# Merge and MLP tail of a two-block model: pair sums on GpSimd, norms as steps between products, the last 512 tokens as two quarters

## The chip, the cores and the metric

One core of one Trainium2 chip runs the whole program. The metric is device time in microseconds (us), the median of the runs shown. TensorE is PE in the rows, VectorE DVE, ScalarE ACT, GpSimd POOL, and SP is the queue of SyncE, which issues most of the DMAs.

## The reference, cut to what matters

The model has two blocks on 1024 tokens of width 1024, all in float32. The change touches only the end of the second block: the gated merge of four branches, and the MLP.

```python
merged = jnp.zeros_like(x)
for i in range(N_BRANCHES):                       # 4 branches of width 256
    gate = jax.nn.sigmoid(h @ w_gate[i] + b_gate[i])
    merged = merged + gate * (branches[i] @ w_branch_up[i])
x = x + rms_norm(merged @ w_out, norm_mix_post)
h2 = rms_norm(x, norm_mlp_pre)
u = jax.nn.relu(h2 @ w_mlp_in)                    # 1024 -> 4096
x = x + rms_norm((u * u) @ w_mlp_out, norm_mlp_post)
```

## The kernel before

Activations are kept transposed: a page is 128 features by 512 tokens, so the 1024 tokens are two halves, and a matrix of width 1024 is 8 pages in each half. Float32 accuracy comes from splitting each operand into a high and a low part in a faster matmul format. `split` (L101) writes the high part on ACT and the low part (source minus high) on DVE; `mm3` (L111) then makes three matmuls of each product (lines L113, L114, L115). A product of one output page from 8 weight blocks, which `fm` (L167) makes, is so 24 matmuls of 512 columns. Weights come in pieces of 128 x 1024 by `wload` (L144): a DMA into one of two `raw` buffers, then the split into one of two `whi` and two `wlo`.

`merge` (L1755) works as follows. `branch_parts` (L1743) loads the 8 pages that the branches left in DRAM for one half into buffers named Y and splits them into pages named H (32 of them in all). Then `up(f)` makes output page f of the half, for f from 0 to 7: `gates` (L1764) loads the four gate pages of the NEXT f into Y buffers, four short products (6 matmuls each) go to PSUM, DVE multiplies each with (1 + gate) (L1780) into a further Y buffer and adds it to the sum so far (L1782), and the sum is split (L107 on ACT, L108 on DVE) into M pages. There are 16 Y buffers. The first half's eight `up` run alone; the second half's eight `up` alternate with the eight `proj` (L1788) of the first half, each 24 matmuls with `w_out2`, whose result ACT copies out and squares for the norm. Then `norms(0)` (L1797), the eight `proj` of the second half, and `norms(1)`.

`norms` needs the sum of squares over features: `rnorm` (L209) sums over partitions with matmuls against a column of ones (L198), takes the power -1/2 on POOL (L141) and spreads the result over the partitions with further matmuls (L206). Then for each of 8 pages: load the old page (tag `xo`, two buffers, L1802), scale (L1803), add the old page on DVE (L1804), store (L1805). `norm_half` (L807) squares the new pages, makes a second `rnorm`, and `h_pages` (L216) scales and splits each into H pages, the input of the MLP.

`fill` (L942) makes left-over gate products where TensorE would wait. When `merge` begins, two are left, and `self.fill(2)` at L1811 uses them up, so the `self.fill(1)` in the loop finds none, before the change as after it.

`mlp` (L1825) goes through the 32 hidden pages in 8 chunks of 4: `hidden` makes a chunk's pages (24 matmuls per page and half, then ReLU squared and a split), `project` (L1849) multiplies them with `w_mlp_out` and adds into 16 Y pages (L1862). The last chunk goes half by half: while `hidden` of the second half runs, `finish(0)` (L1870) norms the first half's output and stores it (L1883), in four steps between the four products. After the last product `finish(1)` does the same for the second half, with nothing beside it.

The program is written in the order above, but the order on each engine is made by a scheduler that lists an instruction as soon as its inputs and its buffer are due by its own reckoning, earlier program text first. Each engine, and SP, then works through its list in order: an instruction whose input is late holds up what stands behind it.

## Time and profile before

| what | us |
|---|---|
| median of 3 runs (3504.82 to 3507.55) | 3505.5 |
| the profiled execution, its own time | 3508.32 |
| its span, first to last instruction | 3506.5 |
| merge, first `up` to the MLP's first stretch without a wait (2572.9 to 2810) | 237.1 |
| MLP from there to the last matmul (2810 to 3486.1) | 676.1 |
| after the last matmul (3486.1 to the end) | 20.4 |

The page lists TensorE as busy 96% of the span. The times of one stretch are read as follows: the matmuls in it, times the distance at which they follow each other where nothing holds them up, against the length of the stretch; the difference is what TensorE lost there.

### The profile page before, as it was taken

What the parts mean: (1) busy time and instruction counts of PE and PEld (TensorE: products, weight loads), DVE (VectorE), ACT (ScalarE), POOL (GpSimd) and SP (SyncE); (2) the same over time, 40 slices, a digit from 0 to 9 for tenths busy, and PEclk for the clock granted to TensorE, in tenths of its full rate; (3) what the DMA queues carried; (4) which work ended last, traced back from release to release, by engine and by line L of the source; (5) the groups of instructions that cost most, each with busy time, mean ns of one, the idle gap of its engine ahead of it and who ended that gap; (6) DMA issues with size and microseconds to landing.
All of it is one profiled execution on the core that took longest, in us unless ns stands there. A gap on an engine that the chain in (4) does not pass through costs nothing.

```text
span 3506.5 us, 45207 instructions
## 1 busy us (share of the span) xinstructions
PE 3369.9 (96%) x18181; PEld 2812.7 (80%) x18181; DVE 1966.9 (56%) x3418; ACT 1321.3 (38%) x2106; POOL 109.2 (3%) x132
## 2 busy tenths in 40 slices
PE   7999999999999999999999999999989899999997
PEld 5888988777888888787777777779768788888886
DVE  6767644556767644565664367453477743333336
ACT  4656412334655312443312345463233442222222
POOL 0000000000000000000100000000000000000000
PEclk9999999999999999999999999999999999999998
DMA  5111111452111111443231211122275421111114
GB/s 185 57 36 51 50 55 57 140 179 86 48 43 36 41 46 63 158 162 119 87 95 65 67 55 56 49 70 75 85 256 178 158 89 48 48 49 49 49 61 149
DMA packets 138707, 302.34 MB, mean 86 GB/s; under 512 B 23944, under 2 KB 41336, under 8 KB 137984
## 3 DMA queue, kind: packets, MB, share of 16 engines
q1 hardware_dynamic: 129280, 282.65, 24.7%
q10 hardware_dynamic: 9216, 16.78, 1.3%
q8 instruction: 143, 2.34, 0.3%
q14 instruction: 68, 0.56, 0.1%
HBM read 245.30 MB, written 58.28 MB: 87 GB/s over the span
## 4 chain that ended last, share of the span: by engine, by line
PE 83%; DVE 5%; issue 5%; ACT 3%; DMA 3%; POOL 1%; SPq 0%; DVEq 0%; POOLq 0%; ACTq 0%
PE mm L113 21%; PE mm L114 21%; PE mm L115 21%; PE lg L388 2%; PE lg L389 2%; PE tp L512 2%; PE pv L113 1%; PE pv L206 1%; PE pv L114 1%; PE pv L115 1%; DMA S<-mix 1%; PE tp L198 1%; DVE wlo L105 1%; PE tp L1392 1%; ACT whi L104 1%
## 5 line engine op out<-in xcount | busy, mean ns | idle before, releaser
L113 PE MATMUL mm<-H,whi 128*128 128x512 f32 x2400 | 958.2, 400 | 26.9 <-DVE S L369 5.0
L115 PE MATMUL mm<-H,wlo 128*128 128x512 f32 x2400 | 949.4, 396 | 5.9 <-DVE wlo L105 5.7
L114 PE MATMUL mm<-H,whi 128*128 128x512 f32 x2400 | 949.8, 396 | 2.1 <-DVE H L105 2.1
L104 ACT CAST whi<-raw 128x1024 fp32r<-128x1024 f32 (+1 forms) x340 | 334.4, 984 | 860.3 <-PE mm L114 768.7
L105 DVE TENSOR_TENSOR wlo<-raw,whi 128x1024 fp32r<-128x1024 f32 (+1 forms) x340 | 387.4, 1140 | 421.6 <-ACT whi L104 409.9
L113 PEld LDWEIGHTS mm<-H,whi 128*128 128x128 f32 x2400 | 456.5, 190 | 125.5 <-ACT H L107 7.2
L115 PEld LDWEIGHTS mm<-H,wlo 128*128 128x128 f32 x2400 | 455.7, 190 | 104.2 <-DVE wlo L105 12.3
L114 PEld LDWEIGHTS mm<-H,whi 128*128 128x128 f32 x2400 | 456.2, 190 | 92.7 <-DVE H L105 2.9
L113 PE MATMUL mm<-whi,H 128*128 128x256 f32 x960 | 277.2, 289 | 3.9 <-DVE S L576 3.2
L114 PE MATMUL mm<-wlo,H 128*128 128x256 f32 x960 | 274.6, 286 | 3.1 <-DVE wlo L105 3.1
L115 PE MATMUL mm<-whi,H 128*128 128x256 f32 x960 | 273.7, 285 | 0.0
L113 PE MATMUL mm<-M,whi 128*128 128x512 f32 x640 | 249.5, 391 | 1.7 <-ACT whi L104 1.5
L115 PE MATMUL mm<-M,wlo 128*128 128x512 f32 x640 | 249.7, 390 | 0.2 <-DVE wlo L105 0.2
L114 PE MATMUL mm<-M,whi 128*128 128x512 f32 x640 | 249.5, 390 | 0.0
L113 PEld LDWEIGHTS mm<-whi,H 128*128 128x128 f32 x960 | 184.6, 192 | 6.8 <-issue 4.2
L114 PEld LDWEIGHTS mm<-wlo,H 128*128 128x128 f32 x960 | 184.8, 193 | 5.1 <-DVE wlo L105 4.2
L115 PEld LDWEIGHTS mm<-whi,H 128*128 128x128 f32 x960 | 184.6, 192 | 0.4
L489 DVE CUSTOM_DVE_ANT_0 lg<-lg,strip 128x1024 f32<-128x1024 f32 x128 | 155.2, 1234 | 25.8 <-PE lg L389 25.6
L1862 DVE TENSOR_TENSOR Y<-Y,mm 128x512 f32<-128x512 f32 x112 | 77.0, 687 | 159.1 <-PE mm L115 159.0
L493 ACT ACTIVATE L<-lg,mx 128x1024 f32<-128x1024 f32 x128 | 142.7, 1118 | 36.5 <-DVE mx L489 30.3
L113 PEld LDWEIGHTS mm<-M,whi 128*128 128x128 f32 x640 | 120.2, 188 | 28.0 <-ACT whi L104 1.9
L115 PEld LDWEIGHTS mm<-M,wlo 128*128 128x128 f32 x640 | 120.5, 188 | 25.6 <-DVE wlo L105 0.6
(455 smaller groups left out, 4968.0 us busy)
## 6 DMA issues: line engine op xcount, KB each, us to landing
raw<-in_w_in SPq DMA_DIRECT2D x106, 512.0 KB, 3.6
raw<-in_w_out SPq DMA_DIRECT2D x48, 512.0 KB, 4.0
raw<-in_w_gate SPq DMA_DIRECT2D x46, 512.0 KB, 3.5
raw<-in_w_mlp_in SPq DMA_DIRECT2D x40, 512.0 KB, 3.3
raw<-in_w_mlp_out SPq DMA_DIRECT2D x40, 512.0 KB, 3.2
Y<-gates SPq DMA_DIRECT2D x64, 256.0 KB, 5.0
gates<-gs ACTq DMA_DIRECT2D x60, 256.0 KB, 2.0
mix<-S SPq DMA_DIRECT2D x48, 256.0 KB, 2.1
```

The source lines that it names most:

```text
L104: nc.scalar.copy(hi, src)
L105: nc.vector.tensor_tensor(out=lo, in0=src, in1=hi.bitcast(F32), op=ALU.subtract)
L113: mm(out, lh, rh, start=start, stop=False)
L114: mm(out, lh, rl, start=False, stop=False)
L115: mm(out, ll, rh, start=False, stop=stop)
L198: self.nc.tensor.matmul(ss[:, n * i + j:n * i + j + 1], acc[:, j * P:(j + 1) * P], self.one, start=True, stop=True)
L388: mm(out, Q[m][qb // 4][:, sl], KH[m][half][:, o:o + kn], start=True, stop=False)
L389: mm(out, Q[m][qb // 4][:, sl], KL[m][half][:, o:o + kn], start=False, stop=not more)
L489: nc.vector.tensor_tensor_reduce(out=lg, in0=lg, in1=strip[:, w0:w0 + 1024], op0=ALU.add, op1=ALU.min, scale=-1.0, scalar=3.0e38, accum_ou ...
L493: nc.scalar.activation(pm, lg, AF.Exp, bias=mx, scale=-1.0, accum_out=sm)
L512: nc.tensor.transpose(tp[:, j, :], pm[:, kb * P:(kb + 1) * P], self.ident)
L1862: nc.vector.tensor_tensor(out=Y[d][half], in0=Y[d][half], in1=pt, op=ALU.add)
```

## The change

Seven things change, all in `merge` and `mlp`:

- `up` multiplies in place, in the gate's own Y buffer. Products 1 and 3 are added to 0 and 2 on GpSimd, and DVE adds the two pair sums. Each `up` so asks for 4 Y buffers in place of 8.
- The old pages of a half are fetched into 8 H buffers by `olds`, and no longer through 2 `xo` buffers.
- `norms` becomes ten steps (`first`, four `add`, `second`, four `scale`); the add of the old page moves to GpSimd, and the squares are taken page by page.
- The first half's steps run between the `proj` of the second half, as (3, 2, 0, 1, 1, 1, 1, 1) after each; the second half's run in the MLP, between the products of `hidden` and `project` of chunk 0 of the first half.
- `finish` takes the statistics in its first step, works on any columns of a half, and sends every second output page from ACT's queue.
- The last weights (4 pieces) are split into H pages (`last_weights`), not into `whi` and `wlo`.
- The last half's products are made for 256 tokens, then for the other 256, with the norm of the first quarter in steps inside the second.

```diff
@@ -180,12 +180,12 @@
             self.mm3(out, xh[:, sl], xl[:, sl], w[k][0], w[k][1], k == 0, k == nk - 1)
-    def sumsq_add(self, acc, src, first, scale=1.0, tag=("sq", 2)):
+    def sumsq_add(self, acc, src, first, scale=1.0, tag=("sq", 2), n=512):
         nc = self.nc
         if first:
             nc.scalar.activation(acc, src, AF.Square, scale=scale)
         else:
-            t = self.T(*tag)
+            t = self.T(*tag)[:, 0:n]
             nc.scalar.activation(t, src, AF.Square, scale=scale)
             nc.vector.tensor_tensor(out=acc, in0=acc, in1=t, op=ALU.add)
@@ -1756,7 +1756,7 @@
         nc = self.nc
-        res = []
+        res = [{} for _ in range(8)]
         M = [{} for _ in range(8)]
         G = {}
@@ -1772,17 +1772,16 @@
             hs = slice(half * 512, half * 512 + 512)
             gates(half * 8 + f + 1)
             w = self.wload(self.seg("w_up", f * 1024, 8, 128), 8, 128)
-            acc = None
-            for i, g in enumerate(G.pop(half * 8 + f)):
+            ts = G.pop(half * 8 + f)
+            for i, t in enumerate(ts):
                 pt = self.ps("mm")
                 self.fm(pt, w[2 * i:2 * i + 2], B[i], half)
-                t = self.T("Y", 16)
-                nc.vector.scalar_tensor_tensor(out=t, in0=g, scalar=1.0, in1=pt, op0=ALU.add, op1=ALU.mult)
-                if acc is not None:
-                    nc.vector.tensor_tensor(out=t, in0=t, in1=acc, op=ALU.add)
-                acc = t
+                nc.vector.scalar_tensor_tensor(out=t, in0=t, scalar=1.0, in1=pt, op0=ALU.add, op1=ALU.mult)
+                if i % 2:
+                    nc.gpsimd.tensor_tensor(out=t, in0=t, in1=ts[i - 1], op=ALU.add)
+            nc.vector.tensor_tensor(out=ts[3], in0=ts[3], in1=ts[1], op=ALU.add)
             hi, lo = self.T("M", 32, F32R), self.T("M", 32, F32R)
-            self.split(hi, lo, acc, scale=0.5)
+            self.split(hi, lo, ts[3], scale=0.5)
             M[f][half] = (hi, lo)
         def proj(f, half, ys, acc):
@@ -1794,16 +1793,37 @@
             self.sumsq_add(acc, y, f == 0)
             ys.append(y)
-        def norms(half, ys, acc):
+        def olds(half):
+            xo = [self.hp.tile([P, 512], F32, tag="H", bufs=32, name=self.nm("xo")) for _ in range(8)]
+            for f in range(8):
+                nc.sync.dma_start(out=xo[f], in_=self.x2[f * P:(f + 1) * P, half * 512:half * 512 + 512])
+            return xo
+
+        def norms(half, ys, acc, xo):
+
             hs = slice(half * 512, half * 512 + 512)
-            r = self.rnorm(acc, 1.0 / 1024.0)
-            for f in range(8):
-                xo = self.T("xo", 2)
-                nc.sync.dma_start(out=xo, in_=self.x2[f * P:(f + 1) * P, hs])
-                nc.vector.scalar_tensor_tensor(out=ys[f], in0=ys[f], scalar=self.n2[:, 8 + f:9 + f], in1=r, op0=ALU.mult, op1=ALU.mult)
-                nc.vector.tensor_tensor(out=ys[f], in0=ys[f], in1=xo, op=ALU.add)
-                nc.sync.dma_start(out=self.x3[f * P:(f + 1) * P, hs], in_=ys[f])
-            res.append(self.norm_half(ys, self.n2[:, 16:24]))
+            r = []
+
+            def first():
+                r.append(self.rnorm(acc, 1.0 / 1024.0))
+
+            def add(f0):
+                if f0 == 0:
+                    r.append(self.T("acc", 2))
+                for f in (f0, f0 + 1):
+                    nc.vector.scalar_tensor_tensor(out=ys[f], in0=ys[f], scalar=self.n2[:, 8 + f:9 + f], in1=r[0], op0=ALU.mult, op1=ALU.mult)
+                    nc.gpsimd.tensor_tensor(out=ys[f], in0=ys[f], in1=xo[f], op=ALU.add)
+                    nc.sync.dma_start(out=self.x3[f * P:(f + 1) * P, hs], in_=ys[f])
+                    self.sumsq_add(r[1], ys[f], f == 0)
+
+            def second():
+                r.append(self.rnorm(r[1], 1.0 / 1024.0))
+
+            def scale(f0):
+                for f in (f0, f0 + 1):
+                    res[f][half] = self.h_pages(ys[f], r[2], self.n2[:, 16 + f:17 + f])
+            pairs = range(0, 8, 2)
+            return [first] + [lambda f=f: add(f) for f in pairs] + [second] + [lambda f=f: scale(f) for f in pairs]
         ys, accs = [[], []], [self.T("yacc", 2) for _ in range(2)]
         B = self.branch_parts(br, 0)
@@ -1811,18 +1831,19 @@
         self.fill(2)
         for f in range(8):
             up(f, B, 0)
-            self.fill(1)
+            self.fill((1, 1, 1, 1, 1, 2, 1, 0)[f])
         B = self.branch_parts(br, 1)
         for f in range(8):
             up(f, B, 1)
             proj(f, 0, ys[0], accs[0])
-        norms(0, ys[0], accs[0])
+        steps = deque(norms(0, ys[0], accs[0], olds(0)))
         for f in range(8):
             proj(f, 1, ys[1], accs[1])
-        norms(1, ys[1], accs[1])
-        return self.pair_halves(res)
-
-    def mlp(self, H, out):
+            for _ in range((3, 2, 0, 1, 1, 1, 1, 1)[f]):
+                steps.popleft()()
+        return res, norms(1, ys[1], accs[1], olds(1))
+
+    def mlp(self, H, steps, out):
         nc = self.nc
@@ -1842,11 +1863,11 @@
                     hi, lo = self.T("M", 32, F32R), self.T("M", 32, F32R)
                     self.split(hi, lo, t)
                     U[j][half] = (hi, lo)
-                if between:
-                    between[j]()
+                for fn in between[j:j + 1]:
+                    fn()
             return U
-        def project(ch, U, halves):
+        def project(ch, U, halves, between=()):
             for dp in range(4):
                 w = self.wload(self.seg("w_mlp_out", (ch * 4 + dp) * 1024, 4, 256), 4, 256)
                 for dd in range(2):
@@ -1860,6 +1881,8 @@
                             nc.scalar.copy(Y[d][half], pt)
                         else:
                             nc.vector.tensor_tensor(out=Y[d][half], in0=Y[d][half], in1=pt, op=ALU.add)
+                for fn in between[dp:dp + 1]:
+                    fn()
         def olds(half):
             X = [self.T("M", 32) for _ in range(8)]
@@ -1867,30 +1890,66 @@
                 nc.sync.dma_start(out=X[d], in_=self.x3[d * P:(d + 1) * P, half * 512:half * 512 + 512])
             return X
-        def finish(half, X):
-
-            hs = slice(half * 512, half * 512 + 512)
-            acc = self.T("yacc", 2)
+        def finish(half, X, c0=0, n=512):
+
+            cs, os = slice(c0, c0 + n), slice(half * 512 + c0, half * 512 + c0 + n)
+            acc = self.T("yacc", 2)[:, 0:n]
             for d in range(8):
-                self.sumsq_add(acc, Y[d][half], d == 0)
-            r = self.rnorm(acc, 1.0 / 1024.0)
+                self.sumsq_add(acc, Y[d][half][:, cs], d == 0, n=n)
+            r = []
             def scale(d0):
+                if d0 == 0:
+                    r.append(self.rnorm(acc, 1.0 / 1024.0))
                 for d in (d0, d0 + 1):
-                    y = Y[d][half]
-                    nc.vector.scalar_tensor_tensor(out=y, in0=y, scalar=self.n2[:, 24 + d:25 + d], in1=r, op0=ALU.mult, op1=ALU.mult)
-                    nc.vector.tensor_tensor(out=y, in0=y, in1=X[d], op=ALU.add)
-                    nc.sync.dma_start(out=out[d * P:(d + 1) * P, hs], in_=y)
+                    y = Y[d][half][:, cs]
+                    nc.vector.scalar_tensor_tensor(out=y, in0=y, scalar=self.n2[:, 24 + d:25 + d], in1=r[0], op0=ALU.mult, op1=ALU.mult)
+                    nc.vector.tensor_tensor(out=y, in0=y, in1=X[d][:, cs], op=ALU.add)
+                    (nc.scalar if d % 2 else nc.sync).dma_start(out=out[d * P:(d + 1) * P, os], in_=y)
             return [lambda d=d: scale(d) for d in range(0, 8, 2)]
-        for ch in range(last):
-            for halves in ((0,), (1,)) if ch == 0 else ((0, 1),):
-                project(ch, hidden(ch, halves), halves)
+        def last_weights():
+
+            W = []
+            for dp in range(4):
+                raw = self.wp.tile([P, 4, 256], F32, tag="raw", bufs=N_RAW, name=self.nm("raw"))
+                nc.sync.dma_start(out=raw, in_=self.seg("w_mlp_out", (last * 4 + dp) * 1024, 4, 256))
+                W.append([])
+                for k in (0, 2):
+                    hi, lo = (self.hpage().rearrange("p (k n) -> p k n", n=256) for _ in range(2))
+                    self.split(hi, lo, raw[:, k:k + 2, :])
+                    W[dp] += [(hi[:, i, :], lo[:, i, :]) for i in range(2)]
+            return W
+
+        def quarter(W, U, half, c0, steps):
+            cs = slice(c0, c0 + 256)
+            Uq = [{half: tuple(t[:, cs] for t in u[half])} for u in U]
+            for d in range(8):
+                pt = self.ps("mm")[:, 0:256]
+                self.fm(pt, [tuple(t[:, d % 2 * P:d % 2 * P + P] for t in w) for w in W[d // 2]], Uq, half)
+                y = Y[d][half][:, cs]
+                nc.vector.tensor_tensor(out=y, in0=y, in1=pt, op=ALU.add)
+                if d in (2, 3, 4, 5) and steps:
+                    steps[d - 2]()
+
+        def both(*fns):
+            def run():
+                for fn in fns:
+                    fn()
+            return run
+
+        U = hidden(0, (0,), [both(*steps[0:3]), both(*steps[3:5]), both(), steps[5]])
+        project(0, U, (0,), steps[6:])
+        project(0, hidden(0, (1,)), (1,))
+        for ch in range(1, last):
+            project(ch, hidden(ch, (0, 1)), (0, 1))
         project(last, hidden(last, (0,)), (0,))
         U = hidden(last, (1,), finish(0, olds(0)))
-        X = olds(1)
-        project(last, U, (1,))
-        for fn in finish(1, X):
+        X, W = olds(1), last_weights()
+        quarter(W, U, 1, 0, ())
+        steps = finish(1, X, 0, 256)
+        quarter(W, U, 1, 256, steps)
+        for fn in finish(1, X, 256, 256):
             fn()
     def second_block(self, H, out, end_banks):
@@ -1922,8 +1981,8 @@
                 self.fill(len(self.fills) - NLATE)
             end_banks()
             with self.banks("tail", 4, 0, 1, 2), self.phase("tail"):
-                H2 = self.merge(brd)
-                self.mlp(H2, out)
+                H2, steps = self.merge(brd)
+                self.mlp(H2, steps, out)
 def _woff():
```

## Rows read from the trace of the kernel before

**Rows 1.** Stretches: PE, PEld, DVE, ACT, POOL busy (instructions), PEclk, DMA share, GB/s

```profile
2572.90:2621.60 48.70, 45.29 (x192) 35.48 (x192) 47.03 (x70) 14.89 (x21) 0.00 (x0) 1.00 0.88 306
2621.60:2628.20 6.60, 0.75 (x3) 0.19 (x2) 6.34 (x10) 2.82 (x5) 0.00 (x0) 0.92 0.94 311
2628.20:2634.20 6.00, 6.00 (x14) 4.50 (x15) 5.96 (x10) 3.64 (x8) 0.00 (x0) 0.52 0.94 357
2634.20:2720.90 86.70, 86.70 (x384) 71.57 (x382) 62.75 (x86) 30.84 (x40) 0.00 (x0) 1.00 0.51 164
2720.90:2760.00 39.10, 34.29 (x155) 27.50 (x155) 27.76 (x41) 17.59 (x27) 2.01 (x2) 0.96 0.55 176
2760.00:2810.00 50.00, 45.89 (x208) 36.68 (x207) 38.19 (x57) 23.42 (x36) 2.01 (x2) 0.97 0.47 157
2810.00:3440.00 630.00, 629.85 (x2778) 520.91 (x2776) 241.61 (x304) 152.65 (x210) 0.00 (x0) 1.00 0.18 60
3440.00:3463.70 23.70, 22.86 (x101) 18.61 (x100) 17.66 (x27) 6.47 (x9) 1.01 (x1) 0.93 0.46 158
3486.10:3506.50 20.40, 3.14 (x17) 2.75 (x16) 11.71 (x19) 0.63 (x1) 1.01 (x1) 0.61 0.27 103
```

**Rows 2.** DVE in order of time, inside one `up` of the first half

```profile
2601.39 1.22 DVE L105 TENSOR_TENSOR wlo<-raw,whi 128x1024 fp32r<-128x1024 f32 x1
2602.53 0.68 DVE L1782 TENSOR_TENSOR Y<-Y,Y 128x512 f32<-128x512 f32 x1
2603.13 1.87 DVE L1780 SCALAR_TENSOR_TENSOR Y<-Y,mm 128x512 f32<-128x512 f32 x3
2604.93 0.68 DVE L108 SCALAR_TENSOR_TENSOR M<-Y,M 128x512 fp32r<-128x512 f32 x1
```

**Rows 3.** TensorE's waits, 2621.6 to 2634.2: total us, times, longest

```profile
PE mm L113 <- ACT H L104: 3.7, 1, 3.7
```

**Rows 4.** SP's queue in order of time: start, us, line, transfer

```profile
2585.42 0.90 SPq L1802 DMA_DIRECT2D xo<-x  x2
...
2621.16 3.97 SPq L1750 DMA_DIRECT2D Y<-br  x8
```

**Rows 5.** GpSimd's groups by shape, whole span: count, busy us, mean ns, idle before

```profile
L141 POOL TENSOR_TENSOR l<-l,mhalf 128x16 f32<-128x16 f32 x4 | 12.4, 3111 | 141.0 <-DVE l L140 141.0
L362 POOL MEMSET S<- 64x512 f32 x16 | 8.3, 521 | 17.1 <-PE lg L388 6.3 <-DVE N L219 3.3 <-ACT L L104 2.9
```

**Rows 6.** TensorE's waits, 2720.9 to 2760: total us, times, longest

```profile
PE tp L198 <- DVE acc L190: 1.8, 1, 1.8
PE pv L206 <- POOL rn L141: 1.3, 2, 0.8
```

**Rows 7.** TensorE's waits, 2760 to 2810

```profile
PE mm L115 <- DVE wlo L105: 1.8, 1, 1.8
```

**Rows 8.** DVE's waits, 2720.9 to 2810

```profile
DVE Y L1804 <- DMA xo<-x: 4.9, 6, 1.5
```

**Rows 9.** TensorE in order of time: the first norm's sums over partitions

```profile
2720.87 1.05 PE L198 MATMUL tp<-one,yacc 128*128 128x1 f32 x8
2721.78 0.48 PE L114 MATMUL mm<-M,whi 128*128 128x512 f32 x1
```

**Rows 10.** One stretch of products with 256 columns (columns as in the first group)

```profile
2434.60:2457.20 22.60, 22.60 (x190) 22.60 (x190) 1.18 (x2) 2.96 (x5) 0.00 (x0) 1.00 0.15 48
```

**Rows 11.** TensorE in order of time, after the last product: the norm's broadcast

```profile
3490.89 2.08 PE L206 MATMUL pv<-c_ident,rn 128*128 128x128 f32 x8 [1.41 <-POOL rn L141]
```

**Rows 12.** DVE's groups by line, 3486 to the end

```profile
L1881 DVE SCALAR_TENSOR_TENSOR Y<-Y,n,pv 128x512 f32<-128x512 f32 x8 | 5.6, 741 | 3.3 <-PE pv L206 3.3
L1882 DVE TENSOR_TENSOR Y<-Y,M 128x512 f32<-128x512 f32 x8 | 5.1, 683 | 0.0
```

**Rows 13.** DVE's groups by shape, whole span: operations of 256 columns

```profile
L584 DVE TENSOR_TENSOR S<-S,qd 128x256 f32<-128x256 f32 x32 | 13.4, 419 | 0.3
L1728 DVE SCALAR_TENSOR_TENSOR gS<-gS,gcd,kvm 128x256 f32<-128x256 f32 x16 | 7.7, 481 | 0.2
```

## The prediction

> **What bounds the kernel now.** I read the stretches first [rows 1], then what ends the waits inside the bad ones. In a stretch without waits 384 matmuls of 512 columns take 86.7 us, 0.226 us each, at full clock. Against that the MLP from 2810 to 3440 loses almost nothing: TensorE is busy 629.85 of 630.00 us, and nothing is to be had there. What is lost in the code that changes lies in four places:
>
> - First half's `up` and its end, 2572.9 to 2634.2, 61.3 us: 192 + 3 + 14 = 209 matmuls should take 47.2 us, so 14.1 us are lost, 5.3 of them in the eight `up` (48.7 less 192 x 0.226 = 43.4) and 8.8 behind them.
> - First norm beside the second half's `proj`, 2720.9 to 2760: 155 PE instructions less 32 of the norms are 123, 27.8 us of 39.1: 11.3 lost.
> - Second norm beside the first MLP products, 2760 to 2810: 176, 39.7 us of 50.0: 10.3 lost.
> - After the last product: 20.4 us, nothing beside it.
>
> In the `up`, DVE is the bound: busy 47.0 of 48.7 us [rows 1]. Starts in order of time give what each operation holds it for [rows 2]: a `wlo` 1.14 us (2601.39 to 2602.53), a sum 0.60, a gate product 0.60 (three from 2603.13 to 2604.93), and the low part of M I take at 0.60 too. One `up` has one `wlo`, three sums, four gate products, one low part: 1.14 + 1.80 + 2.40 + 0.60 = 5.94 us, where its 24 matmuls need 5.42. Behind the `up`, TensorE waits 3.7 us for the first H page of the second half [rows 3]: its source pages are asked for only at 2621.16 [rows 4], as the last `up` ends, because each `up` takes 8 of the 16 Y buffers and the branch pages get theirs when the last gates have been read. Then TensorE runs at 0.52 of its clock, the lower of its two levels, 1.2 GHz, for 6.0 us after an idle 6.6 [rows 1]: some 2.9 us more.
>
> **The change, part by part.** Sums are made against the profiled execution, 3508.3 us, which stands 2.8 above the median 3505.5; the gain is then taken off the median.
>
> *Pair sums on GpSimd.* DVE loses two of three sums: 5.94 - 1.20 = 4.74 us per `up`, under TensorE's 5.42. GpSimd gains two adds of 128x512 per `up`. No row shows such an add. Its nearest rows are a memset of 512 columns, 0.52 us, and a power on 128x16, 3.1 us [rows 5]. The memset only writes; an add reads two operands and writes one. I bound it by one and three such passes, 0.52 to 1.56 us, and take two, 1.04, since it has the memset's width and the power's price belongs to another function. Whether DVE can work beside it is not shown either: bounds are none of it and all of it holding DVE up. I take half, as 2.40 of DVE's 4.74 us are gate products that read one operand from PSUM: 4.74 + 2 x 1.04 / 2 = 5.78 us, 0.36 over TensorE, 2.9 us in eight `up`. The last sum on DVE now waits for GpSimd, and behind it in DVE's list stand the next `wlo` and gate products, for which TensorE waits through its four PSUM banks; the other half of the adds is what I leave for that wait to hide in. In the second half's `up`, DVE has 86.7 - 62.8 = 24 us free [rows 1]: nothing there.
>
> The Trainium skill (GPSIMD Engine Reference, section 3.1) gives 4497 ns for an add of 2048 float32 columns; a quarter is an estimate of 1.12 us, with which the sum would come out 0.6 us later. No run here shows it.
>
> *In-place gates.* An `up` asks for 4 Y buffers, so the branch pages of the second half can be asked for some two `up` sooner, and the 8.8 us behind the `up` should mostly go. Next late is DVE: eight low parts of H pages at 0.60, 4.8 us, with no free time on DVE if the `up` cost 5.78. I let these 4.8 us stand, and no drop of the clock. Sum of this place: 2.9 + 4.8 = 7.7 lost in place of 14.1, **a gain of 6.4**. Ends: with no blocking DVE has 43.4 - 37.9 = 5.5 us free and hides the 4.8, but the DMA does not: up to 2628.2 it moved 306 x 48.7 + 311 x 6.6 = 17.0 MB [rows 1], less 0.5 for two old pages that went early [rows 4], and 16.5 MB at 357 GB/s, the highest of these stretches, take 46.2 us, 2.8 over TensorE; gain 11.3. With 1.56 us all blocking, an `up` takes 7.86, eight lose 19.5, and with 4.8 and 2.9 of clock the loss is 27.2: 13.1 worse than now.
>
> *Old pages by eights, norms in steps.* A norm's own matmuls stay: eight take 0.91 us [rows 9], four such groups in each stretch 3.6, so 7.7 + 6.7 = 14.4 us are waits and slow clock. Of these the waits for GpSimd's power, 1.3 in the first stretch [rows 6] and, at the longest of these, 0.8 in the second, stay, since DVE, GpSimd and TensorE still take turns. The other 12.3 come from DVE's list: it stands 4.9 us before L1804 for old pages that two buffers let in late [rows 8], and behind it the accumulations and `wlo`, for which TensorE waits 1.8 and 1.8 [rows 6, 7]. With eight pages fetched ahead and the add on GpSimd, DVE no longer waits for them; the 16 loads stay on SP, asked for earlier; one whose H buffer is late would hold the pieces of weights behind it, for which I count nothing, as the first half's 16 H pages are read to the end before the second half's `up`. New is that the squares wait for GpSimd's add, and the power stands behind the adds in GpSimd's list. I take three quarters of 12.3, **9.2**. Ends: all of it, 12.3, and nothing: 16 adds that block DVE for 1.04 are 16.6 us against DVE's 23 us free in the two stretches [rows 1].
>
> *Two quarters.* After the last product: 16 scale operations of 512 columns, 741 and 683 ns [rows 12], become 481 and 419 [rows 13]: 8 x 0.52 = 4.2 us. The broadcast, 2.08 [rows 11], halves: 1.04. So does the sum over partitions: 0.5. Three operations on the way to it (add, square, accumulate) lose 0.25 each: 0.75. Together 6.5. Against it: 192 matmuls of 256 columns follow at 22.6 / 190 = 0.119 us, weight loads filling all of that time [rows 10]; 192 x 0.119 - 96 x 0.226 = 1.2. A second set of norm matmuls among products: 1.0. Its wait and clock: I take 1.5, between nothing and the 2.7 which the stretch from 3440 loses beyond its 0.226 x (101 - 16) and its 1.8 of norm matmuls [rows 1]. **Net 2.8**, ends 1.6 and 4.3. The first half's `finish` keeps that stretch as it is.
>
> *At nothing:* splitting the last weights into H pages is the same work in smaller pieces, beside `hidden`, where DVE is busy 17.7 of 23.7 us and ACT 6.5 [rows 1]; without that cover it would cost up to four `wlo`, 4.6. Of the stores, 12 go to ACT's queue, 8 of them the last half's (now 16 of half size): an ACT that waits to issue one holds the cast of a `whi` behind it, which ACT's idle time hides. The fills are the same in both.
>
> Sum: 6.4 + 9.2 + 2.8 = 18.4 us; 3508.3 becomes 3489.9, and the median 3487.
>
> **The rivals.**
>
> - *GpSimd's adds hold DVE for their whole 1.04 us.* `up` takes 6.82: 11.2 lost, with 4.8 and 2.9 of clock 18.9, 4.8 worse than now; 9.2 and 2.8 stay: 3498.3. For it: DVE's list has three operations of two SBUF operands in each `up`; against it, the gate products between them. The Trainium skill (SBUF — State Buffer, "Who interferes with whom") says that a DVE instruction with two SBUF inputs and a GpSimd instruction that reads SBUF shut each other out for a whole instruction; by that rule this case or the last one decides, and no trace here has both at once.
> - *The transfers bound the boundary.* They fill 0.88 and 0.94 of the DMA engines' time [rows 1]. At the 308 GB/s of these stretches 16.5 MB take 53.6 us: 10.2 lost and 2.9 of clock; gain 1.0 there: 13.0 in all, 3492.5.
> - *The steps do not land where they stand.* The order on the engines is not the program's: an old page is asked for at 2585.42 [rows 4], 140 us before its norm. If the steps land as the norms do now, only the 4.9 us of old pages go: 6.4 + 4.9 + 2.8 = 14.1, 3491.4.
> - *Slower: one GpSimd add stops DVE for p over 1.5 us.* Then eight `up` lose 8 x (4.74 + 2p - 5.42) + 7.7; all gains, 14.1 + 9.2 + 2.8 = 26.1, are used up at p = 1.49. At p = 2.0 it is 34.3, 8.2 slower, 3514. The bound of three passes, 1.56, just reaches it; the 3.1 us row says that GpSimd can be slow, the memset row against it.
>
> **How the numbers follow.** Chances: forecast 0.62, whole blocking 0.12, transfers 0.10, steps 0.08, slower 0.08. A difference of 0.2%, 7 us, is about what a measurement of this kernel can tell from no change. Faster is under 3498.5: nearly all of the forecast, transfers and steps, half of whole blocking: 0.82; within, 0.10; slower 0.08. Range: the best ends give 11.3 + 12.3 + 4.3 = 27.9, 3477.6, and I go to 3475 for a price below one of mine; above, it takes in whole blocking with an end of another term: 3502.
>
> **What would show it.** Right: eight `up` in 44 to 47 us, GpSimd adds near 1 us, no low clock behind them, no DVE wait for an old page, the two norm stretches together losing under 14, and 14 us after the last product. Wrong: DVE operations of two SBUF operands longer than 0.69 or idle before them, with GpSimd as releaser; branch pages still asked for after the last `up`; new waits of TensorE for `wlo` or accumulations beside the norms.

## The result and the profile after

The changed kernel takes 3532.4 us (median of four, 3530.8 to 3539.6) against 3505.2 for the kernel before in the same comparison: ratio 1.0077, interval 1.0065 to 1.0090, slower. The forecast was 3487, faster. The profiled execution took 3530.8 us, its span is 3528.8.

I compare the traces at equal work: the time at which TensorE has done as many columns of products as the kernel before had at 2573, 2690, 2850 and 3420 us, and at its last product. The table gives how much longer each stretch lasts than before, in us (negative: shorter); the MLP from 2850 to 3420 differs by 0.1 at most and is left out. The runs e1 to f5 are the experiments of the next section. The column of the ups reaches to 2690, into the ups of the second half. "Ahead" is all that lies before the merge, where the instruction lists are the same as before.

| run | ahead | ups and their end | two norms | 3420 to last product | behind it | sum without ahead |
|---|---|---|---|---|---|---|
| forecast | 0 | -6.4 | -9.2 | +3.7 | -6.5 | -18.4 |
| after | -2.5 | +8.2 | +10.6 | +10.8 | -4.8 | +24.8 |
| e1_dve_up | -5.0 | +7.3 | +10.2 | +11.3 | -4.8 | +24.1 |
| e2_dve_old | -6.1 | +7.7 | +8.6 | +9.2 | -4.8 | +20.6 |
| e3_separate | -1.0 | -1.7 | +9.7 | +11.0 | -4.8 | +14.2 |
| e4_w_first | -1.1 | +6.3 | +9.7 | +3.7 | -4.8 | +14.9 |
| e5_w_gate | +1.1 | +2.8 | +10.8 | +9.0 | -4.7 | +17.8 |
| e6_burst | +4.4 | -0.2 | +11.0 | +3.6 | -4.8 | +9.6 |
| e7_spread_dve | +1.3 | -1.8 | -3.1 | +2.4 | -4.9 | -7.4 |
| e8_spread | +5.1 | -1.0 | -3.1 | +2.5 | -5.2 | -6.8 |
| e9_late_scale | +8.6 | -1.3 | -3.2 | +2.4 | -6.8 | -8.8 |
| e10_branch_early | -1.1 | +3.4 | -3.2 | +3.9 | -5.1 | -1.0 |
| e11_raw_ahead | -0.3 | +4.0 | +10.6 | +10.0 | -5.2 | +19.5 |
| e12_all | +4.1 | +2.8 | -4.8 | +4.2 | -6.7 | -4.5 |
| f1_spread_again | +1.9 | -0.6 | -1.8 | +2.4 | -4.9 | -4.8 |
| f2_late_again | -7.9 | -1.9 | -3.2 | +2.1 | -6.6 | -9.5 |
| f3_late_dve_pairs | +1.7 | -1.9 | -3.2 | +2.5 | -6.1 | -8.8 |
| f4_defer | +2.4 | -2.1 | -3.1 | +2.4 | -6.5 | -9.2 |
| f5_pool_all | +4.3 | +6.6 | -4.8 | +3.9 | -6.8 | -1.0 |

Rows with the same program text in a stretch (f1 is e7's kernel again, f2 is e9's) show how far a stretch varies by itself: the ups as changed lose 6.3 to 8.2 (after, e2, e4), with separate buffers they gain 0.2 to 1.9 (e3, e6 to e9, f1, f2), the norms as changed lose 9.7 to 10.8 (after, e1, e3, e4, e5, e11), and from 3420 to the last product 9.0 to 11.3 are lost (after, e1, e2, e3, e5, e11). Behind the last product such rows differ by 0.7 at most. Only a difference that is clear of this is called shown below.

The stretches of the profile after, columns as in [rows 1]. The first does the work of the first three there (67.4 us in place of 61.3; the other 2 of the 8.2 us lie behind it), the second is a part of it, the third to fifth are the two norms and the MLP, the sixth is new, the two quarters, and the last is what stands behind the last product:

```profile
2570.50:2637.90 67.40, 55.44 (x208) 41.51 (x209) 51.33 (x70) 21.44 (x31) 26.56 (x16) 0.91 0.80 273
...
2589.20:2597.00 7.80, 7.76 (x21) 5.74 (x22) 3.76 (x5) 1.04 (x1) 1.04 (x1) 0.62 0.65 248
...
2726.50:2770.30 43.80, 36.23 (x155) 29.49 (x155) 26.56 (x33) 17.90 (x27) 16.09 (x10) 0.88 0.34 109
2770.30:2826.50 56.20, 48.05 (x207) 38.92 (x206) 38.97 (x51) 23.32 (x35) 16.38 (x10) 0.91 0.46 150
2826.50:3456.50 630.00, 629.85 (x2778) 521.18 (x2777) 241.08 (x302) 152.87 (x210) 0.00 (x0) 1.00 0.20 60
3480.70:3512.90 32.20, 26.99 (x199) 26.04 (x198) 20.17 (x48) 9.22 (x20) 0.69 (x1) 0.89 0.38 129
3512.90:3528.80 15.90, 2.43 (x10) 1.88 (x9) 9.57 (x27) 1.25 (x3) 0.70 (x1) 0.62 0.27 90
```

DVE is busy 51.3 of 67.4 us in the ups and their end, before 59.3 of 61.3, and no engine is full: the changed stretches wait. Behind the longest wait in the ups TensorE also runs at 0.62 of its clock for 7.8 us. Its waits in three windows, the ups, the norms and the last two stretches (us in total, times, longest):

```profile
PE mm L113 <- ACT whi L104: 6.4, 2, 5.9
...
PE mm L113 <- ACT whi L104: 4.7, 1, 4.7
PE mm L115 <- DVE wlo L105: 4.2, 1, 4.2
...
PE mm L113 <- ACT H L104: 4.9, 2, 4.6
PE tp L198 <- DVE yacc L190: 3.8, 1, 3.8
```

The first and the fourth come out of SP's queue. What it issues there in order of time, at the ups, at the quarters, and, last, at the ups before the change (start, us):

```profile
2567.88 12.73 SPq L1769 DMA_DIRECT2D Y<-gates  x16
2580.67 0.42 SPq L153 DMA_DIRECT2D raw<-in_w_up  x1
...
3482.12 5.01 SPq L1890 DMA_DIRECT2D M<-x  x8
3487.23 0.38 SPq L1916 DMA_DIRECT2D raw<-in_w_mlp_out  x1
```
```profile
2570.38 5.00 SPq L1769 DMA_DIRECT2D Y<-gates  x8
2576.40 1.01 SPq L153 DMA_DIRECT2D raw<-in_w_up  x2
```

Sixteen gate pages, before eight, are asked for ahead of the third piece of `up` weights, eight old pages ahead of the fourth piece of last weights. Buffers were free for those pages, so they went first, and what TensorE needed next came late. The second wait comes out of ACT's list in the second norm, where squares that wait for GpSimd's adds stand ahead of the weight cast:

```profile
2804.12 0.63 ACT L189 ACTIVATE sq<-Y 128x512 f32<-128x512 f32 x1 [1.78 <-POOL Y L1815]
2807.06 0.63 ACT L189 ACTIVATE sq<-Y 128x512 f32<-128x512 f32 x1 [2.31 <-POOL Y L1815]
2807.59 1.03 ACT L104 CAST whi<-raw 128x1024 fp32r<-128x1024 f32 x1
```

### The profile page after: what moved, and what is told of

Read it like the earlier page. It is cut to its first block, busy times and chain, and to the rows that moved or that the text cites. A ratio compares the mean times of both kernels' runs of the same rounds, so it can differ in the third digit from the quotient of the medians.

```text
span 3528.8 us, 45539 instructions
## 1 busy us (share of the span) xinstructions
PE 3378.2 (96%) x18277; PEld 2823.2 (80%) x18277; DVE 1962.9 (56%) x3406; ACT 1324.0 (38%) x2118; POOL 187.3 (5%) x181
## 5 line engine op out<-in xcount | busy, mean ns | idle before, releaser
L113 PE MATMUL mm<-M,whi 128*128 128x512 f32 x608 | 238.7, 394 | 4.8 <-ACT whi L104 4.7
L115 PE MATMUL mm<-M,wlo 128*128 128x512 f32 x608 | 238.9, 393 | 4.6 <-DVE wlo L105 4.6
L114 PE MATMUL mm<-M,whi 128*128 128x512 f32 x608 | 238.8, 393 | 0.0
L141 POOL TENSOR_TENSOR rn<-rn,mhalf 128x4 f32<-128x4 f32 (+1 forms) x35 | 42.2, 1206 | 1924.9 <-DVE rn L140 1364.2
```

The costliest lines, as they stand in the source:

```text
L113: mm(out, lh, rh, start=start, stop=False)
L114: mm(out, lh, rl, start=False, stop=False)
L115: mm(out, ll, rh, start=False, stop=stop)
L141: nc.gpsimd.tensor_tensor(out=out, in0=out, in1=self.mhalf[:, 0:n], op=ALU.pow)
```

## The experiments

**The ups: SP's queue or GpSimd.** Theory: SP's queue. Rival: the adds on GpSimd stop DVE. First the adds back on DVE:

```diff
-                    nc.gpsimd.tensor_tensor(out=t, in0=t, in1=ts[i - 1], op=ALU.add)
+                    nc.vector.tensor_tensor(out=t, in0=t, in1=ts[i - 1], op=ALU.add)
```

> The changed kernel, with the pair sums of the up products on DVE again, still in place in the gates' buffers. Measured against the kernel before, counted at equal matmul work, the changed kernel lost 8.5 us in the first half's up stage, 6.1 of them in one wait for the third piece of w_up, which stands behind 16 gate pages in SP's list. Theory A (SP's list, made longer by the Y buffers that in-place gates set free): the 16 gate pages stand ahead of that piece here too, so the wait stays, 4 us or more, and the stage stays 5 to 9 us worse than before. Theory B (GpSimd's adds block DVE): the stage comes back to within 2 us of the kernel before. All other stages as in the changed kernel within 1 us.

Measured 3527.7 us; the ups lose 7.3 in place of 8.2, within what the stretch varies by. Then the adds left on GpSimd and the gates no longer in place, so that an `up` takes eight Y buffers again:

```diff
-                nc.vector.scalar_tensor_tensor(out=t, in0=t, ...
+                g, t = t, self.T("Y", 16)
+                ts[i] = t
+                nc.vector.scalar_tensor_tensor(out=t, in0=g, ...
```

> The changed kernel, but each gate product goes to a Y buffer of its own as before; the pair sums stay on GpSimd. SP's list in the up stage is then that of the kernel before. Theory A (SP's list): the wait for the third piece of w_up goes, and the stage is within 2 us of the kernel before, or a gain; GpSimd's adds stay at 1.3 to 2.1 us. Theory B (GpSimd's adds block DVE): the stage stays 6 us or more worse than before. In both, the branch pages of the second half are asked for as late as before, so the wait behind the last up is back, 4 to 7 us.

Measured 3521.6 us; SP asks for eight gate pages (2569.39, 4.99 us) and then for the weights, and the ups take 1.7 us less than before. With the adds on GpSimd the loss is gone, so they do not make it. It remained to show that the order does it, with gates in place. Weights ahead of the next gates, 12 pages in front:

```diff
-            gates(half * 8 + f + 1)
             w = self.wload(self.seg("w_up", f * 1024, 8, 128), 8, 128)
+            gates(half * 8 + f + 1)
```

> The changed kernel, whole, but each up asks for its weights before the next gates, so that 12 gate pages instead of 16 stand ahead of the third piece of up weights in SP's list. Theory (SP's list makes the loss in the up stage): sixteen pages took 12.73 us to issue there, so four fewer bring that piece some 3.2 us sooner, TensorE's wait for it falls from 6.1 to about 3 us, and the time from 3530.8 to about 3527.6. Rival (the adds on GpSimd make that loss by stopping DVE): the wait stays at 6 us, 3530 to 3531.

Measured 3527.4 us; the ups and their end lose 2.8 in place of 8.2. SP's queue there:

```profile
2571.49 8.65 SPq L1769 DMA_DIRECT2D Y<-gates  x12
2582.74 0.33 SPq L153 DMA_DIRECT2D raw<-in_w_up  x1
```

That the whole time met the expected 3527.6 is luck: the ups gained 5.4 us and not 3.2, and the part ahead stood 3.6 later. And the weights asked for one piece ahead, 8 pages in front:

```diff
-            gates(half * 8 + f + 1)
-            w = self.wload(...)
+            w = self.wload(..., raw=R.pop(0) if R else None)
+            if half == 0:
+                if f < 7:
+                    R.append(self.raw_up(f + 1))
+                gates(f + 1)
```

> The changed kernel, whole, but the up weights are asked for one piece ahead in the first half, so that 8 gate pages stand ahead of the third piece instead of 16 (12 in the run with weights ahead of the next gates). Theory (SP's list): TensorE's wait for that piece, 6.1 us with 16 pages, falls to at most 1 us, the up stage takes 2 to 3 us less than with 12 pages, about 3524.5. Rival (adds on GpSimd): the stage stays as with 12 pages, 3527.

Measured 3527.7 us, not 3524.5. The eight ups lose nothing any more, but behind them TensorE waits 9.7 us once, for the first weights of the second half. SP's queue in that trace, as above:

```profile
2601.73 10.72 SPq L1775 DMA_DIRECT2D Y<-gates  x8
2612.54 8.64 SPq L1756 DMA_DIRECT2D Y<-br  x8
...
2624.88 0.42 SPq L159 DMA_DIRECT2D raw<-in_w_up  x1
```

The buffers that in-place gates set free went to gates of later ups, eight of them ahead of the branch pages, and these stand ahead of the second half's weights. So I asked for the branch pages in four pieces, on the kernel of e7 below:

```diff
             self.fill((1, 1, 1, 1, 1, 2, 1, 0)[f])
-        B = self.branch_parts(br, 1)
+            if f > 3:
+                B1 += self.branch_parts(br, 1, (f - 4,))
```

> The run with spread steps on DVE, but the second half's branch pages are asked for in four pieces, behind the first half's fifth to eighth up, and not all behind the eighth. Theory (the two waits behind the eighth up, some 6 us, come from pages that are asked for late): they fall to 2 or 3 us, 3 to 4 us gained between 2600 and 2640. Rival (transfers bound this place: the DMA engines are 0.91 busy in the ups): the same wait appears at the gates or weights of the last ups, 0 to 1 us gained.

Measured 3506.4 us: 5.2 worse at this place than e7. The waits come earlier, for DVE's gate products (3.1 us) and weights (1.8), and 3.0 for an H page stays. Theory (3 to 4 us gained) and rival (0 to 1 gained) both missed the size. The waits moved as the rival said; that transfers do it is not shown.

**The norms: adds, fetching or steps.** Their adds back on DVE, on the kernel after:

```diff
-                    nc.gpsimd.tensor_tensor(out=ys[f], in0=ys[f], in1=xo[f], op=ALU.add)
+                    nc.vector.tensor_tensor(out=ys[f], in0=ys[f], in1=xo[f], op=ALU.add)
```

> The changed kernel, with the add of the old page in the merge's norms on DVE; the steps and the eight prefetched pages stay. The changed kernel lost 4.6 us beside the first norm and 6.0 beside the second against the kernel before. Theory A (GpSimd's adds of 1.6 us are late for the squares on ACT, and stop DVE; what stands behind them, wlo and whi, is late): both stages come back and gain what was forecast, 3 to 5 us each against the kernel before, so 8 to 10 us each against the changed kernel for the two together 14 to 20. Rival (where the steps were put costs the time, whoever adds): the two stages together stay 5 us or more worse than before. The GpSimd power beside a wlo stays at 1.9 us in both.

Measured 3522.9 us; the norms lose 8.6 in place of 10.6. The adds are 1 to 2 us of the loss (9.7 to 10.8 with them on GpSimd), not the 14 to 20 of the theory. Then no steps, both norms in one piece, with the eight pages fetched ahead (and e3's buffers, e2's adds, e4's order):

```diff
-        steps = deque(norms(0, ys[0], accs[0], olds(0)))
+        for fn in norms(0, ys[0], accs[0], olds(0)):
+            fn()
...
```

> Old pages fetched by eights, but both norms run in one piece as before, their adds on DVE; the up stage with a separate output buffer (adds of pairs on GpSimd), last weights asked for ahead of the last old pages. Theory (the two norm stretches lose because five steps stand within two products, and not because of the prefetch or the adds): the norm stretches cost no more than before, 3500 to 3504. Rival (the prefetch itself, whose pages take H buffers and stand in SP's list, makes the loss): the 9 us at the norms stay, about 3512.

Measured 3522.2 us: the theory fell, 11.0 lost. DVE's list in that kernel, second norm, from the first scale up to the weight split for which TensorE waits:

```profile
2787.76 1.41 DVE L1816 SCALAR_TENSOR_TENSOR Y<-Y,n,pv 128x512 f32<-128x512 f32 x2 [2.34 <-PE pv L206]
...
2797.29 0.69 DVE L1817 TENSOR_TENSOR Y<-Y,xo 128x512 f32<-128x512 f32 x1
2797.89 1.40 DVE L1816 SCALAR_TENSOR_TENSOR Y<-Y,n,pv 128x512 f32<-128x512 f32 x2
2799.21 0.69 DVE L190 TENSOR_TENSOR acc<-acc,sq 128x512 f32<-128x512 f32 x1
2799.81 1.29 DVE L1817 TENSOR_TENSOR Y<-Y,xo 128x512 f32<-128x512 f32 x2
2801.01 0.69 DVE L1865 SCALAR_TENSOR_TENSOR M<-M 128x512 f32<-128x512 f32 x1
2801.61 0.69 DVE L190 TENSOR_TENSOR acc<-acc,sq 128x512 f32<-128x512 f32 x1
2802.22 1.22 DVE L105 TENSOR_TENSOR wlo<-raw,whi 128x1024 fp32r<-128x1024 f32 x1
```

TensorE's waits there, 2715 to 2820:

```profile
PE mm L115 <- DVE wlo L105: 12.0, 2, 6.6
```

The same norm in the kernel before:

```profile
2779.66 1.41 DVE L1803 SCALAR_TENSOR_TENSOR Y<-Y,n,pv 128x512 f32<-128x512 f32 x2 [2.34 <-PE pv L206]
...
2790.01 1.22 DVE L105 TENSOR_TENSOR wlo<-raw,whi 128x1024 fp32r<-128x1024 f32 x1
2791.15 0.68 DVE L1804 TENSOR_TENSOR Y<-Y,xo 128x512 f32<-128x512 f32 x1
...
2795.41 1.22 DVE L105 TENSOR_TENSOR wlo<-raw,whi 128x1024 fp32r<-128x1024 f32 x1
...
2797.81 0.69 DVE L1804 TENSOR_TENSOR Y<-Y,xo 128x512 f32<-128x512 f32 x1 [0.58 <-DMA xo<-x]
```

With all pages there, the list holds the norm's work in one block ahead of the split, 14.5 us from the first scale on, and there is no wait for a page left in it. Before, two buffers let the pages in one by one [rows 8], the first split stood 10.4 us behind the first scale, and further splits stood between the adds. That fetching by eights makes the block is read from the two lists and not shown by a run of its own: e6 also takes the squares page by page, and no run parts the two. So with steps, spread one to a product:

```diff
-            for _ in range((3, 2, 0, 1, 1, 1, 1, 1)[f]):
+            for _ in range((1, 1, 1, 1, 1, 1, 2, 2)[f]):
...
-        U = hidden(0, (0,), [both(*steps[0:3]), both(*steps[3:5]), both(), steps[5]])
-        project(0, U, (0,), steps[6:])
+        U = hidden(0, (0,), [both(*steps[0:2]), steps[2], steps[3], steps[4]])
+        project(0, U, (0,), [steps[5], steps[6], both(*steps[7:9]), steps[9]])
```

> As the run with the norms in one piece, but with the norms in steps, one step a product (the second norm: two steps at its first and its seventh place), adds on DVE. Theory (steps are good where they are spread: a product of 24 matmuls takes 5.4 us, and one step of two pages gives DVE 3.7 us beside its own 1.7): the norm stretches lose less than before, 3497 to 3502. Rival (any step puts work ahead of the products' weight casts): 9 us more than before at the norms, about 3512.

Measured 3502.9 us, 0.9 above the range; the norms gain 3.1 (1.8 in the second execution, f1), 14 us better than in one piece, and only the places of the steps differ. The same with the adds on GpSimd:

> As the run with spread steps on DVE, but with the norms' adds on GpSimd as the change has them. Theory (an add there takes 1.3 us beside idle DVE and up to 2.1 beside a DVE operation on two SBUF operands, and holds that operation as long): 1 to 3 us more than with the adds on DVE. Rival (the adds relieve DVE of 0.6 us for each page): 1 to 4 us less than with the adds on DVE.

Measured 3506.7 us, 3.7 more, but 3.8 of that lies ahead of the merge: the norms take the same. Theory and rival were both wrong; spread out, it does not matter which engine adds. What is left, in TensorE's waits of e7:

```profile
PE pv L206 <- POOL rn L141: 5.3, 4, 1.8
PE mm L113 <- ACT whi L104: 1.8, 3, 0.9
PE mm L115 <- DVE wlo L105: 0.7, 1, 0.7
```

**The quarters.** On the kernel after, last weights asked for ahead of the old pages:

```diff
-        X, W = olds(1), last_weights()
+        W = last_weights()
+        X = olds(1)
```

> The changed kernel with one line turned round: the last four pieces of w_mlp_out are asked for before the eight old pages of the last half, so the fourth piece has one old page ahead of it in SP's list instead of eight. The changed kernel waits 4.6 us for that piece in the first quarter and then runs at the lower clock. Theory A (SP's list again): the wait falls under 1.5 us and the whole kernel gets 4 to 7 us faster. Rival (two raw buffers are too few to hold the last pieces ahead, whatever the list): the wait stays 3 us or more.

Measured 3522.2 us: the wait of 4.6 us is gone, the stretch loses 3.7 in place of 10.8. One old page stands ahead of the fourth piece now:

```profile
3480.82 0.45 SPq L1890 DMA_DIRECT2D M<-x  x1
3482.23 0.33 SPq L1916 DMA_DIRECT2D raw<-in_w_mlp_out  x1
```

Then, on e7, two scale steps of the third quarter behind the fourth's squares:

```diff
-        quarter(W, U, 1, 256, steps)
-        for fn in finish(1, X, 256, 256):
+        quarter(W, U, 1, 256, steps[:2])
+        late = finish(1, X, 256, 256)
+        for fn in steps[2:] + late:
```

> The run with spread steps on DVE, but two of the four scale steps of the third quarter stand behind the squares of the fourth. Theory (in the tail DVE's list holds the fourth quarter's last five accumulations, 2.5 us, behind the third quarter's scales, and TensorE's last sum waits 4.1 us for them): the sum comes 2 to 3 us sooner, the scales left over fit into DVE's idle 3.2 us around the power, and from the last product to the end it takes 13 to 14 us instead of 15.8. Rival (the squares are late because ACT issues stores ahead of them): no change, 15.5 to 16. Single times differ by up to 5 us through the part ahead of the merge, so the stretch decides.

Measured: 14.0 us from the start of the last matmul of a product to the end in place of 15.9, the wait for the last accumulation 1.7 in place of 3.9. The single time, 3509.0, is 8.6 late from the part ahead.

**What pair sums on GpSimd are worth.** e9's kernel with them on DVE again (the edit of e1), and with all three sums on GpSimd:

```diff
-            nc.vector.tensor_tensor(out=ts[3], in0=ts[3], in1=ts[1], op=ALU.add)
+            nc.gpsimd.tensor_tensor(out=ts[3], in0=ts[3], in1=ts[1], op=ALU.add)
```

> The run with two late scale steps, but the sums of pairs on DVE: nothing of the merge is left on GpSimd but the powers. Theory (the adds on GpSimd give the up stage nothing, because DVE's list waits for them 1.2 us in each up, as long as the two sums that they take off it): the stage from 2573 to 2634 takes as long as with the adds on GpSimd, within 1 us. Rival (they do relieve DVE): 2 to 5 us more in that stage, and in the median.

> The run with two late scale steps, but all three sums of an up on GpSimd, in both halves. DVE waits then not for the pair sum but, one gate product later in its list, for the low part of M: behind the fourth gate product come two adds of 1.28 us and a cast of 0.57, 3.2 us with their handing over, of which the weight split and one gate product cover 1.74. Theory (DVE's own work and the wait in its list make the period): 4.14 of work and about 1.5 of wait are 5.6 to 5.7 us in place of 6.0, the ups get 2 to 3 us shorter. Rival (transfers set the end of this place): then the waits behind the eighth up grow by that, and the stretch from 2573 to 2634 of the kernel before takes as long as with one sum on DVE, within 1 us.

Measured: the ups and their end take 1.9 less than before with the sums on either engine (f3's median is 3506.1, ratio 0.9990, 0.9982 to 0.9999), and 6.6 more with all on GpSimd, where theory and rival both fell (median 3510.8, ratio 1.0003, 0.9992 to 1.0014). The eight ups of three kernels, with none, two and three sums on GpSimd (columns as in [rows 1]):

```profile
2574.00:2622.00 48.00, 45.30 (x194) 35.40 (x193) 46.83 (x70) 15.45 (x21) 0.00 (x0) 1.00 0.87 303
```
```profile
2565.20:2613.20 48.00, 45.13 (x192) 35.28 (x192) 38.77 (x56) 14.72 (x21) 25.23 (x14) 1.00 0.89 301
```
```profile
2577.40:2629.90 52.50, 45.46 (x192) 35.27 (x192) 35.68 (x49) 14.62 (x20) 31.77 (x21) 1.00 0.80 274
```

What DVE waits for in the second and in the third of them:

```profile
DVE Y L1784 <- POOL Y L1783: 8.6, 7, 1.5
```
```profile
DVE M L108 <- ACT M L107: 13.1, 5, 2.6
```

DVE works less from one kernel to the next, and the ups get no shorter: 46.8, 38.8 and 35.7 us busy in 48.0, 48.0 and 52.5. The wait in DVE's list is 1.2 us an `up` with two sums, just what they take off it, and 2.6 with three. I had reckoned 1.5, since the add that runs beside a weight split takes 2.27 and not 1.28. The DMA engines are less busy there, 0.80 against 0.89, so the transfers do not lengthen it. I also wrote each up's last sum behind the next up's second gate product:

```diff
+                if i == 1 and ends:
+                    ends.pop()()
...
-            nc.vector.tensor_tensor(out=ts[3], in0=ts[3], in1=ts[1], op=ALU.add)
+            ends.append(end)
```

> The run with two late scale steps, but in the first half each up's last sum and split stand behind the second gate product of the next up, so that DVE no longer waits for GpSimd's pair sum. Theory (the wait of 1.2 us in DVE's list is why the adds on GpSimd give nothing): the period of an up falls from 6.0 us towards TensorE's 5.4, and the stretch of the ups gets 3 to 4 us shorter. Rival (the transfers set the end of this place: 0.9 busy): the ups get shorter, but the waits behind the eighth get as much longer, and the stretch from 2573 to 2634 as before's rows count it, ups and their end together, changes by less than 1 us. The run with pair sums on DVE has shown 0 us between the two engines.

It kept its place in DVE's list, and the wait its 1.17 to 1.19 us; so the run says nothing of either theory (median 3504.0, ratio 0.9981, 0.9972 to 0.9990). An order that does without the wait was not found.

**Together.** All mends at once, but gates in place (the edits of e11, e10, e2, e7, e4 and e9):

> All mends together on the changed kernel: up weights one piece ahead with gates in place and pair sums on GpSimd, branch pages in four pieces, norms in spread steps with their adds on DVE, last weights ahead of the last old pages, two scale steps of the third quarter late. If each mend does what its own run says and they add up: the ups and their end 3 to 5 us better than before, norms 3, tail 4, together 10 to 12 us under the kernel before, 3495 to 3499. Rival (in-place gates hold DVE, since the sum of pairs waits for GpSimd in DVE's list): no better than the run with spread steps, 3500 to 3503.

Measured 3508.0, above both ranges: the norms gain 4.8 and 6.7 are gained behind the last product, but 4.2 are lost from 3420 on and 2.8 in the ups. Whether in-place gates or the branch pages in four pieces lose there is not told apart; e10 lost 3.4 with the pieces and without gates in place. The best by its stretches so far is e9's kernel. It and e7's were timed again, twelve and eleven times:

> The run with spread steps on DVE once more, now timed in rounds. Its one look gave 3502.95, its stretches from the up stage on 7.7 us less than before, while the part ahead of the merge, whose lists are the same, stood 1.8 us later. Theory (that part varies from execution to execution): the median lies 5 to 8 us under the kernel before, 3498 to 3501. Rival (that part is set when a kernel is built, so the looks' offsets repeat): 3502 to 3504, 2 to 4 us under.

> The run with two late scale steps once more, timed in rounds. Its one look gave 3509.0, its stretches from the up stage on 9.1 us less than before, the part ahead of the merge 8.6 us later. Theory (that part varies from execution to execution): about 2 us under the run with spread steps, 3495 to 3499. Rival (it is set when a kernel is built): again 3507 to 3510, no gain on the kernel before.

Measured for e7's: 3506.6 against 3509.6, ratio 0.9996 (0.9987 to 1.0005; the two medians alone make 0.9991), no difference. For e9's: 3504.5 against 3509.6, ratio 0.9982 (0.9973 to 0.9992), faster than the kernel before by 0.2%, and than the changed one by 0.9% if the two ratios are set against each other. f3's and f4's ratios, 0.9990 and 0.9981, cannot be told from it. Neither median lies in a range expected: 3506.6 is above both of its ranges, 3504.5 between the two. The part ahead of the merge stood 8.6 us late in e9's first execution and 7.9 early in this profile, and the twelve times of that kernel go from 3491.3 to 3510.8: it varies from execution to execution, which is why the stretches and not the single times decide above.

## Why the prediction was wrong

- **In-place gates (gain 6.4 with the pair sums; measured a loss of 8.2).** The step that failed is "so the branch pages of the second half can be asked for some two `up` sooner". Free buffers go to whatever SP's list asks for first, and that was 16 gates; I followed which buffers came free but not who stood ahead in the queue. The branch pages were asked for at 2617.54, 47.0 us behind the stretch's start, before at 48.3.
- **Pair sums on GpSimd.** An add takes 1.3 us alone and 1.5 on average, against 1.04 taken and 1.56 as the bound. The term of half blocking came out near the mark for a wrong reason: 5.78 forecast, 6.0 measured (f2), and not from blocking. The step that failed is leaving the wait of the last sum to hide in "the other half of the adds"; it stands in DVE's list at its full 1.2 us. So the engine of the pair sums made no difference (f2 and f3), and the loss of this place is that of the gates' order. The slower rival gave its sign but its mechanism did not decide: an add lengthens a DVE operation in the ups by 1.1 us at most (a low part of M 1.81 for 0.68), and the gate products not at all.
- **Norms (gain 9.2; measured a loss of 10.6).** DVE no longer waits for old pages, as forecast. The step that failed is that those 4.9 us made TensorE's waits: they spread the norm's work out. With the waits gone and the norms in one piece, 11.0 us are lost (e6); the work stands in one block, and the change's steps, five in two products, kept it close together. That the waits had spread it is read from the lists. "New is that the squares wait for GpSimd's add" was given no price: in the changed kernel's second norm TensorE waits 4.7 us behind such squares, though with the adds on DVE other waits take most of that place (8.6 lost). Spread, the gain is 1.8 to 4.8 in ten runs, mostly 3.1, of 12.3 taken as avoidable. The waits for the power, taken as 1.3 and 0.8, are 5.3 in e7: the power rose from 1.01 [rows 1] to 1.86 to 1.96 us where a weight split now runs beside it.
- **Quarters (gain 2.8; measured a loss of 6.0).** "At nothing" for the last weights failed; its reason looked at the work on DVE and ACT, not at SP's queue: with two buffers and eight old pages ahead the fourth piece came 4.6 us late. With the order mended the gain is 1.1 (4.8 less 3.7), in e9 4.4. Of the 6.5 behind the last product 4.8 came; the rest was DVE doing the third quarter's scales first, and came in e9.
- **The rivals** asked which engine or transfer binds. None asked what a page asked for early stands in front of, which made two of the three losses. The working asked it once, for the norms' old pages ("would hold the pieces of weights behind it, for which I count nothing"), and not for the gates or the last old pages, where it cost the time.

## What to carry over

Before a prefetch is called free, write down what stands behind it in the same queue: a free buffer is filled at once, and pushes back what is needed next. A wait that a change removes may be what spread work out; see where that work goes in the list when nothing holds it any longer. Work handed to another engine saved nothing here, because its result was waited for in the list of the engine that was relieved.

## What was not expected of the hardware

In this trace DVE and GpSimd hold each other up for an operation at a time, but only where DVE reads two operands from SBUF. The groups of the kernel after (min/median/max in ns): gate products, with one operand from PSUM, never stretch, though 19 of the 64 ran beside an add; accumulations from SBUF and the adds themselves do.

```profile
L1779 DVE SCALAR_TENSOR_TENSOR Y<-Y,mm x64: 674/681/689, 2574.6 to 2718.4; 128x512 f32<-128x512 f32 x64
```
```profile
L190 DVE TENSOR_TENSOR acc<-acc,sq x14: 677/884/1775, 2738.4 to 2812.8; 128x512 f32<-128x512 f32 x14
```
```profile
L1781 POOL TENSOR_TENSOR Y<-Y,Y x32: 1260/1295/2288, 2576.0 to 2719.2; 128x512 f32<-128x512 f32 x32
```

That is the rule of the Trainium skill (SBUF — State Buffer, "Who interferes with whom"), and here the trace agrees. Its price of 4497 ns for 2048 columns (GPSIMD Engine Reference, section 3.1), 1.12 us for 512 as an estimate, stands below the 1.26 us of the shortest add.
